# Turning half of a normalised block by VectorE squares and a trip through DRAM in place of TensorE transposes

## The chip, the cores and the metric

The kernel runs on one core of one Trainium2 chip. The time is device microseconds of one execution. The core's engines are TensorE (PE, with its weight loads shown apart as PEld), VectorE (DVE), ScalarE (ACT), GpSimd (POOL) and SyncE (SP); POOL and SP issue the DMAs.

## The reference

One decoder layer on 2048 tokens of width 1024, in float32. The output of the first sub-layer is normalised, modulated, and goes into the second:

```python
        h = x * (1.0 + sc1) + sh1
        z = h @ w_in[l]
        gate_b, gate_c, v_conv, v_pool = jnp.split(z, [CONV_CH, 2 * CONV_CH, 3 * CONV_CH], axis=-1)
        y_conv = gate_b * _short_conv(gate_c * v_conv, conv_w[l])
        y_pool = _multiscale_pool(v_pool, w_pool[l], pool_scale[l])
        mix = jnp.concatenate([y_conv, y_pool], axis=-1) @ w_out[l]
        x = _layer_norm(DEEPNORM_ALPHA * x + (1.0 + g1) * mix, ln1_g[l], ln1_b[l])

        h = x * (1.0 + sc2) + sh2
        f = jnp.square(jax.nn.relu(h @ w_mlp_in[l])) @ w_mlp_out[l]
        x = _layer_norm(DEEPNORM_ALPHA * x + (1.0 + g2) * f, ln2_g[l], ln2_b[l])
```

The hidden width of the second sub-layer is 4096. The convolution, the pooling and the scales from the conditioning vector are small beside the four matrix products.

## The kernel before

The tokens go in two blocks of 1024. In each block the input projection (`in_proj_0`, `in_proj_1`), the output projection (`out_proj`), the up-projection (`up`, eight groups of 512 hidden columns) and the down-projection (`down`) follow each other. A matrix product is made of blocks of half size with seven products in place of eight (sums of blocks stand in for one of them); keys such as "11", "22" or "1" in `ORDER` name the operand block or sum that a product takes. A float32 operand is split by `split` into a high part, cast by ACT, and a low part, subtracted by DVE, and `mm3` makes three matmuls from them. One product of the up-projection is 24 matmuls of 128x128 by 128x512.

`out_proj` gets tokens on partitions: `R[0]` to `R[7]` are eight tiles of 128 tokens by 1024 features, loaded with the residual x and added to. Its operands come from the DRAM tensor `msum` with features on partitions and tokens along the row (`Operands.begin`, `second`, `third`). `normalise` and `scale` centre and scale each finished tile and store it to `nsave`, from which the residual is read later.

The up-projection needs features on partitions again. `turned` does that. `back(0)` turns tiles 0 to 3, 32 transposes of 128x128 by TensorE with an identity, while the last product of `out_proj` runs; the results are operands "11" and "21". `back(1)` turns tiles 4 to 7 in the same way, after the first two products of the first up group; `back(2)` splits operand "22" from it, and `back(3)` to `back(6)` make the sums "1", "2", "3" and "4" with the blocks that `back(0)` stored in `hsave`. In `mlp` the order is: two products of `ups[0]`, `back(1)`, two products of `ups[1]`, `back(2)`, a product of `ups[0]` that takes "22", `back(3)`, a product that takes "1", and so on:

```python
        ups = [up(b, g, B) for g in range(NC)]
        for g in range(2):
            next(ups[g])
            back(1 + g)
        for i in range(3, 7):
            next(ups[0])
            back(i)
```

A scheduler puts each engine's instructions in a fixed order when the program is built, by its own estimate of when data is there; each engine then takes them in that order and waits for semaphores. Tiles come from pools with a fixed number of buffers: ten `o`, five `r`, six `w` and 28 `h` tiles of 1024 columns, and eight PSUM banks `ps`. DMAs that POOL issues take one of eight completion semaphores in turn, and each waits for the last holder of its own.

Of the kernel before, what the change touches and what calls it, by code (L numbers as in the profile page):

```python
# [50 lines left out]
def tile_hybrid_layer(ctx: ExitStack, tc: tile.TileContext, opening, xT, x, wada, win,  # L51
# [20 lines left out]
    def t_o(w=T, dt=F32):  # L72
        return mk(big, [P, w], dt, "o", 10)
# [13 lines left out]
    def split(src, hi, lo):  # L87
        high = nc.scalar.copy(hi, src)  # L88
        return high.ins, nc.vector.tensor_tensor(lo, src, hi.bitcast(F32), op=ALU.subtract).ins  # L89


    def mm3(ps, whi, wlo, xhi, xlo, first, last, goes_on=False):
        nc.tensor.matmul(ps, whi, xhi, start=first, stop=False, skip_group_check=goes_on)  # L93
# [97 lines left out]
    msum = tc.dram_tile([7, NG - 1, P, H], F32, name="msum")  # L191
    wosum = tc.dram_tile([2, 4, P, T], F32, name="wosum")
    udeep = tc.dram_tile([NC, P, 3 * Q], F32, name="udeep")
    wdeep = tc.dram_tile([NC, P, T + 3 * Q], F32, name="wdeep")

    def ada_first():
# [562 lines left out]
    def turned(R):  # L759
        B = {}  # L760
        raw = []

        def operand(key, q, src):
            hi, lo = t_h(), t_h()
            split(src, hi, lo)
            B[key, q] = hi, lo

        def transposed(h, k0, dst):
            for i in range(2):
                k = k0 + i  # L770
                ps = t_ps()
                for t in range(4):
                    nc.tensor.transpose(ps[:, t * P : t * P + P], R[4 * h + t][:, k * P : k * P + P], ident)  # L773
                sc, sh = lng[:, k : k + 1], lnb[:, k : k + 1]
                if h and i:
                    nc.vector.tensor_scalar(dst[:, i * H : i * H + H], ps, sc, sh, op0=ALU.mult, op1=ALU.add)
                else:
                    nc.scalar.activation(dst[:, i * H : i * H + H], ps, AF.Identity, bias=sh, scale=sc)
            return dst

        def back(h):
            if h == 0:
                for q in range(4):
                    r = transposed(0, 2 * q, t_r())
                    nc.gpsimd.dma_start(hsave[q], r)
                    operand("11" if q < 2 else "21", q % 2, r)
            elif h == 1:
                for q in range(2):
                    raw.append((transposed(1, 4 + 2 * q, t_o()), transposed(1, 2 * q, t_o())))
            elif h == 2:  # L790
                for q in range(2):
                    operand("22", q, raw[q][0])
            elif h == 3:
                for q in range(2):
                    b11 = t_o()
                    nc.sync.dma_start(b11, hsave[q])
                    tt(raw[q][1], raw[q][1], b11, ALU.subtract)
                    operand("1", q, raw[q][1])
                    raw[q] = raw[q][0], raw[q][1], b11
            elif h == 4:  # L800
                for q in range(2):
                    tt(raw[q][0], raw[q][0], raw[q][1], ALU.subtract)
                    operand("2", q, raw[q][0])
            elif h == 5:
                for q in range(2):
                    tt(raw[q][2], raw[q][0], raw[q][2], ALU.subtract)
                    operand("3", q, raw[q][2])
            else:
                for q in range(2):
                    b21 = t_o()  # L810
                    nc.sync.dma_start(b21, hsave[2 + q])
                    tt(b21, b21, raw[q][0], ALU.subtract)
                    operand("4", q, b21)

        return B, back

# [3 lines left out]
    class Operands:  # L820
# [10 lines left out]
        def begin(self, n):  # L831
            i = self.index(n)
            r = t_r()
            nc.sync.dma_start(r.rearrange("p (a n) -> p a n", a=2),
                              msum[i, 0:2].rearrange("a p n -> p a n"))
            self.a[n, 0] = parts(r)
            self.weights(n, 0)

        def weights(self, n, g, tile=None):
# [7 lines left out]
        def second(self, n):  # L847
            ns = range(n, min(n + 2, 7))
            r = t_r()
            for i, m in enumerate(ns):  # L850
                self.a[m, 1] = hi, lo = t_h(), t_h()
                nc.sync.dma_start(r[:, halves[i]], msum[self.index(m), 2])
                split(r[:, halves[i]], hi[:, :H], lo[:, :H])

        def third(self, n):
            hi, lo = self.a[n, 1]
            return split(self.mixed[self.index(n)], hi[:, H:], lo[:, H:])

        def whole(self, n):
            self.begin(n)  # L860
# [2 lines left out]
                self.second(n)  # L863
            self.third(n)

    def out_proj(b, ops):
        R, X, Y = [], {}, {}
        B, back = turned(R)
        lo_, hi_ = halves
        mv = {}  # L870
        late, begun = [], []

        def load_x():
            xt = t_o(D)
            nc.gpsimd.dma_start(xt, x[b * T + len(R) * P : b * T + len(R) * P + P, :])
            R.append(xt)

        def matmuls(n, banks, new, ks, then):
            for t in range(4):
                if new and ks[0] == 0:  # L880
# [13 lines left out]

        def end(t, cs, other, scalar=1.0):
            if t not in mv:
                mv[t] = mk(sm, [P, 8], F32, "mv", 8)
            i = 4 + cs.start // H
            begun[:] = [nc.vector.scalar_tensor_tensor(R[t][:, cs], R[t][:, cs], scalar, other, op0=ALU.mult,
                                                       op1=ALU.add, accum_out=mv[t][:, i : i + 1]).ins]  # L900

        def scale():
            t = late.pop()
            begun[:] = [nc.vector.tensor_scalar(R[t], R[t], mv[t][:, 0:1], mv[t][:, 6:7], op0=ALU.add,
                                                op1=ALU.mult).ins]
            nc.gpsimd.dma_start(nsave[t], R[t])

        def normalise(t):
            stats_act(R[t], mv[t])
            if late:  # L910
                scale()
            var_act(mv[t])
            inv_sqrt(mv[t])
            late.append(t)

        def first_row(t, ps):
            end(t, hi_, ps)
            normalise(t)
# [36 lines left out]
        matmuls(6, X, False, every, last_row)  # L955
        scale()
        return B, back

# [540 lines left out]
```

## Time and profile before

| | |
|---|---|
| median of 3 runs | 1734.65 us (1734.5 to 1736.54) |
| span of the profiled execution | 1733.2 us |
| PE busy | 1723.5 us, 7855 matmuls |
| DVE, ACT, POOL busy | 1314.6, 868.1, 205.8 us |
| mean granted TensorE clock | 0.999 |
| DMA moved | 465.24 MB, 268 GB/s |
| the 128 transposes of L773 | 15.6 us of PE |

The profiled execution's own time is given by its span, from its first to its last instruction; the runs' times are a little longer. A row of a timeline has start, duration, engine, line, operation, the tile written and the tiles read, and the shape; x32 means 32 instructions merged. A row of a group has, behind the count, busy time and mean duration in ns, and then the idle time of the engine just ahead of them with what ended it. Matmuls overlap: one lasts 0.39 us but the next starts 0.227 us later. A DMA row has KB and the median time from issue to landing.

### The profile page before, as it was taken

The numbers are of one execution on the slowest core, as the hardware profiler recorded it, in microseconds if no ns is written. First come the engines' busy times: TensorE is split into PE (matmuls) and PEld (weight loads), VectorE is DVE, ScalarE is ACT, GpSimd is POOL, SyncE is SP. The second block draws the span as 40 slices with busy tenths as digits, with TensorE's granted clock in tenths as the row PEclk, the third lists the DMA queues.
The fourth block names the chain that finished last, engine by engine and source line by source line (L and its number), as shares of the span: only waits on it lengthen the run. The fifth ranks groups of instructions, "written<-read, shape, count | busy, mean of one in ns | idle before, by whom it ended". The sixth has DMA issues, their size and how long they took to land.

```text
span 1733.2 us, 21912 instructions
## 1 busy us (share of the span) xinstructions
PE 1723.5 (99%) x7855; PEld 1435.5 (83%) x7855; DVE 1314.6 (76%) x1726; ACT 868.1 (50%) x1172; POOL 205.8 (12%) x399
## 2 busy tenths in 40 slices
PE   9999999999999999999999999999999999999998
PEld 7888888888888888888888888888888889888887
DVE  8897798877777686669686789687566778665896
ACT  6323368554445554446573344775444567444451
POOL 0222220122322000100000000102111110000000
PEclk9999999999999999999999999999999999999999
DMA  9998877778888998887572366657545589777771
GB/s 387 345 337 319 302 267 269 267 262 325 311 326 319 381 418 332 291 286 284 196 271 76 110 219 219 230 185 282 215 179 222 197 290 418 294 273 249 267 264 50
DMA packets 142685, 465.24 MB, mean 268 GB/s; under 512 B 16488, under 2 KB 17008, under 8 KB 142576
## 3 DMA queue, kind: packets, MB, share of 16 engines
q1 hardware_dynamic: 97920, 303.39, 48.0%
q0 software_dynamic: 44656, 160.46, 24.4%
q8 instruction: 61, 1.00, 0.2%
q14 instruction: 48, 0.39, 0.1%
HBM read 318.55 MB, written 145.23 MB: 268 GB/s over the span
## 4 chain that ended last, share of the span: by engine, by line
PE 95%; DMA 3%; issue 1%; DVE 1%; ACT 0%; SPq 0%; POOL 0%; DVEq 0%; POOLq 0%
PE ps L95 30%; PE ps L93 30%; PE ps L94 30%; PE ps L425 3%; DMA r<-in_w 1%; DMA usum<-o 1%; PE ps L773 1%; DVE o L98 0%; DMA o<-in_w 0%; DMA o<-in_opening 0%; DVE w L89 0%; DVE r L98 0%; ACT w L88 0%; DVE o L1369 0%; SPq L108 0%
## 5 line engine op out<-in xcount | busy, mean ns | idle before, releaser
L95 PE MATMUL ps<-h,w 128*128 128x512 f32 x1312 | 510.2, 389 | 0.4 <-DVE w L89 0.4
L94 PE MATMUL ps<-h,w 128*128 128x512 f32 x1312 | 510.3, 389 | 0.0
L93 PE MATMUL ps<-h,w 128*128 128x512 f32 x1312 | 510.0, 389 | 0.0
L93 PE MATMUL ps<-h,h 128*128 128x512 f32 (+1 forms) x1176 | 444.2, 378 | 0.0
L95 PE MATMUL ps<-h,h 128*128 128x512 f32 (+1 forms) x1176 | 444.1, 378 | 0.0
L94 PE MATMUL ps<-h,h 128*128 128x512 f32 (+1 forms) x1176 | 444.0, 378 | 0.0
L88 ACT CAST h<-r 128x1024 fp32r<-128x1024 f32 (+2 forms) x186 | 187.8, 1014 | 298.0 <-PE ps L94 186.8
L95 PEld LDWEIGHTS ps<-h,w 128*128 128x128 f32 x1312 | 246.3, 188 | 52.1 <-DVE w L89 0.8
L94 PEld LDWEIGHTS ps<-h,w 128*128 128x128 f32 x1312 | 246.3, 188 | 51.5 <-DVE h L89 0.5
L93 PEld LDWEIGHTS ps<-h,w 128*128 128x128 f32 x1312 | 246.0, 188 | 51.3 <-ACT h L88 0.2
L89 DVE TENSOR_TENSOR h<-r,h 128x1024 fp32r<-128x1024 f32 (+2 forms) x186 | 217.3, 1173 | 93.5 <-ACT h L88 93.0
L88 ACT CAST w<-r 128x1024 fp32r<-128x1024 f32 x156 | 164.3, 1053 | 242.6 <-PE ps L94 231.3
L89 DVE TENSOR_TENSOR w<-r,w 128x1024 fp32r<-128x1024 f32 x156 | 190.5, 1222 | 96.3 <-ACT w L88 95.4
L94 PEld LDWEIGHTS ps<-h,h 128*128 128x128 f32 x1176 | 221.3, 188 | 41.1
L95 PEld LDWEIGHTS ps<-h,h 128*128 128x128 f32 x1176 | 221.3, 188 | 40.8
L93 PEld LDWEIGHTS ps<-h,h 128*128 128x128 f32 x1176 | 221.3, 188 | 40.5
L98 DVE TENSOR_TENSOR o<-o,o 128x1024 f32<-128x1024 f32 (+2 forms) x193 | 171.1, 890 | 41.0 <-DMA usum<-o 31.8
L98 DVE TENSOR_TENSOR o<-o,ps 128x512 f32<-128x512 f32 (+1 forms) x175 | 113.7, 658 | 54.3 <-PE ps L95 53.4
L89 DVE TENSOR_TENSOR h<-w,h 128x1024 fp32r<-128x1024 f32 x114 | 137.6, 1207 | 4.3 <-ACT h L88 4.1
L88 ACT CAST h<-w 128x1024 fp32r<-128x1024 f32 x114 | 118.6, 1040 | 12.8 <-DMA w<-wdeep 4.1
L1013 POOL DMA_DIRECT2D usum<-o x111 | 59.4, 535 | 472.3 <-ACT o L1010 195.0
L98 DVE TENSOR_TENSOR r<-r,r 128x1024 f32<-128x1024 f32 x60 | 73.4, 1223 | 21.5 <-DMA r<-in_w 17.5
(160 smaller groups left out, 1243.0 us busy)
## 6 DMA issues: line engine op xcount, KB each, us to landing
usum<-o POOLq DMA_DIRECT2D x111, 512.0 KB, 4.8
r<-usum SPq DMA_DIRECT2D x109, 512.0 KB, 5.5
w<-w2sum SPq DMA_DIRECT2D x64, 512.0 KB, 5.9
r<-in_w SPq DMA_DIRECT2D x60, 512.0 KB, 6.0
w<-in_w SPq DMA_DIRECT2D x40, 512.0 KB, 7.4
o<-in_w SPq DMA_DIRECT2D x72, 256.0 KB, 6.4
w2sum<-o POOLq DMA_DIRECT2D x64, 256.0 KB, 6.7
msum<-o POOLq DMA_DIRECT2D x18, 512.0 KB, 4.9
```

Of the source, the lines that this page charges most:

```text
L88: high = nc.scalar.copy(hi, src)
L89: return high.ins, nc.vector.tensor_tensor(lo, src, hi.bitcast(F32), op=ALU.subtract).ins
L93: nc.tensor.matmul(ps, whi, xhi, start=first, stop=False, skip_group_check=goes_on)
L94: nc.tensor.matmul(ps, whi, xlo, start=False, stop=False, skip_group_check=goes_on)
L95: nc.tensor.matmul(ps, wlo, xhi, start=False, stop=last, skip_group_check=goes_on)
L98: return nc.vector.tensor_tensor(out_, a, b_, op=op)
L425: nc.tensor.matmul(ps[m, h], wt[:, w : w + P], A[k][p // 2][:, hs], start=k == 0 and p == 0, stop=k == KD - 1 and p == 2)
L773: nc.tensor.transpose(ps[:, t * P : t * P + P], R[4 * h + t][:, k * P : k * P + P], ident)
L1013: nc.gpsimd.dma_start(usum[g, i], r)
```

## The change

The four tiles of the second half of a block are no longer turned by TensorE. When such a tile is scaled, DVE turns it in squares of 32x32 into four collecting tiles (`blocks`, one for each 256 features), four instructions a tile. After the last tile 16 DMAs store them into the new DRAM tensor `tsave`, in pieces of 512 bytes, and `back(1)` loads them back with features on partitions, four DMAs of 512 KB. Scale and shift by `lng` and `lnb` are then applied to the loaded tile, half by ACT and half by DVE, where they were applied to the PSUM banks.

For the squares to land in token order the rows of an `R` tile are other tokens than before: partition group `a` of tile `t` holds 32 tokens that lie 128 apart from the next group's (`rows_of`). So the tile is loaded and stored by four DMAs of 32 rows each, and the operands from `msum` are split with their columns in another order (`split_rows`, 512 columns at a time). The first half is still turned by TensorE and put back into token order as it leaves PSUM.

```diff
+    def by_rows(ap):
+        return ap.rearrange("p (t a j) -> p a t j", t=4, a=4)
+    def by_tokens(ap):
+        return ap.rearrange("p (a t j) -> p a t j", t=4, a=4)
+    def split_rows(src, hi, lo):
+        for i in range(0, src.shape[-1], H):
+            cs = slice(i, i + H)
+            split(by_tokens(src[:, cs]), by_rows(hi[:, cs]), by_rows(lo[:, cs]))
...
+    tsave = tc.dram_tile([4, 2, P, H], F32, name="tsave")
...
-        def transposed(h, k0, dst):
-            for i in range(2):
+        blocks = []
+
+        def turn(t):
+            if t == 0:
+                blocks.extend(t_o() for _ in range(4))
+            for q, r in enumerate(blocks):
+                nc.vector.transpose(r.rearrange("p (b t j) -> p t b j", b=8, t=4)[:, t],
+                                    R[4 + t][:, q * Q : q * Q + Q].rearrange("p (b j) -> p b j", b=8))
+                if t == 3:
+                    for a in range(4):
+                        own = slice(32 * a, 32 * a + 32)
+                        nc.gpsimd.dma_start(
+                            tsave[q].rearrange("k (q i) (a r) -> a i (k q) r", q=4, a=4)[a],
+                            r[own].rearrange("i (b r) -> i b r", b=8))
+
+        def affine_row(dst, src, k):
+            sc, sh = lng[:, k : k + 1], lnb[:, k : k + 1]
+            nc.scalar.activation(dst, src, AF.Identity, bias=sh, scale=sc)
+
+        def turned_back(k0, dst):
+            nc.gpsimd.dma_start(dst.rearrange("p (k n) -> p k n", k=2), tsave[k0 // 2].rearrange("k p n -> p k n"))
+            for i, hs in enumerate(halves):
                 k = k0 + i
+                if i:
+                    nc.vector.tensor_scalar(dst[:, hs], dst[:, hs], lng[:, k : k + 1], lnb[:, k : k + 1],
+                                            op0=ALU.mult, op1=ALU.add)
+                else:
+                    affine_row(dst[:, hs], dst[:, hs], k)
+            return dst
+
+        def transposed(k0, dst):
+            for i, hs in enumerate(halves):
                 ps = t_ps()
                 for t in range(4):
-                    nc.tensor.transpose(ps[:, t * P : t * P + P], R[4 * h + t][:, k * P : k * P + P], ident)
...
+                    nc.tensor.transpose(ps[:, t * P : t * P + P], R[t][:, (k0 + i) * P : (k0 + i) * P + P], ident)
+                affine_row(by_tokens(dst[:, hs]), by_rows(ps), k0 + i)
...
-                    raw.append((transposed(1, 4 + 2 * q, t_o()), transposed(1, 2 * q, t_o())))
+                    raw.append((turned_back(4 + 2 * q, t_o()), turned_back(2 * q, t_o())))
...
-            self.a[n, 0] = parts(r)
+            self.a[n, 0] = hi, lo = t_h(), t_h()
+            split_rows(r, hi, lo)
...
+    def rows_of(t):
+        for a in range(4):
+            start = t // 4 * H + a * P + t % 4 * 32
+            yield slice(start, start + 32), slice(32 * a, 32 * a + 32)
...
-            nc.gpsimd.dma_start(xt, x[b * T + len(R) * P : b * T + len(R) * P + P, :])
+            for rs, own in rows_of(len(R)):
+                nc.gpsimd.dma_start(xt[own], x[b * T + rs.start : b * T + rs.stop, :])
...
-            nc.gpsimd.dma_start(nsave[t], R[t])
+            for rs, own in rows_of(t):
+                nc.gpsimd.dma_start(nsave[rs.start // P, rs.start % P : rs.start % P + 32], R[t][own])
+            if t >= 4:
+                turn(t - 4)
```

Three places in the built order of block 0, each before and after. First POOL, where the output projection ends and the up-projection begins. Before, `o_1969` to `o_1975` are tiles 4 to 7 and `o_2483` is the first result of the up-projection:

```order
L785 DMA hsave<-r_2325 128x1024
L906 DMA nsave<-o_1969 128x1024
L906 DMA nsave<-o_1971 128x1024
L906 DMA nsave<-o_1973 128x1024
L906 DMA nsave<-o_1975 128x1024
L1013 DMA usum<-o_2483 128x1024
```

After, from the third collecting tile `o_2444` on, with what each row waits for (DMASW0 to DMASW7 are the eight semaphores of POOL's DMAs; the four tiles' stores and the first two collecting tiles' stand ahead of it in the same way). `o_2622` and `o_2630` become operand "22", `o_2626` and `o_2634` operand "1":

```order
L791 DMA tsave<-o_2444 32x8x128 [waits DMASW4_49,DVE_49]
L791 DMA tsave<-o_2444 32x8x128 [waits DMASW5_49]
L791 DMA tsave<-o_2444 32x8x128 [waits DMASW6_49]
L791 DMA tsave<-o_2444 32x8x128 [waits DMASW7_49]
L791 DMA tsave<-o_2445 32x8x128 [waits DMASW0_49,DVE_49]
L791 DMA tsave<-o_2445 32x8x128 [waits DMASW1_49]
L791 DMA tsave<-o_2445 32x8x128 [waits DMASW2_49]
L791 DMA tsave<-o_2445 32x8x128 [waits DMASW3_49]
L1060 DMA usum<-o_2582 128x1024 [waits DMASW4_49,DVE_49,Activation_49]
L800 DMA o_2622<-tsave 128x2x512 [waits DMASW7_49,DMASW6_49,DMASW5_49]
L800 DMA o_2626<-tsave 128x2x512
L800 DMA o_2630<-tsave 128x2x512 [waits DMASW2_49,DMASW3_49,DMASW1_49,DMASW0_49]
```

Between the tiles' stores and the later results there are now 16 stores, one result's store and four loads, and the first load waits for the third collecting tile's stores to land.

Second ACT, at the affine and the cast of operand "22". Before, `o_2523` and `o_2549` are "22", `w_2657` the weight that it is multiplied with, `w_2703` and `w_2748` the next two:

```order
L88 CAST w_2657<-r_2655 128x1024
L778 ACTIVATE o_2523<-ps_2524,lnb,lng 128x512
L1009 ACTIVATE o_2483<-o_2483 128x1024
L778 ACTIVATE o_2536<-ps_2537,lnb,lng 128x512
L1010 ACTIVATE o_2483<-o_2483 128x1024
L778 ACTIVATE o_2549<-ps_2550,lnb,lng 128x512
L778 ACTIVATE o_2562<-ps_2563,lnb,lng 128x512
L88 CAST h_2647<-o_2523 128x1024
L88 CAST h_2651<-o_2549 128x1024
L1000 COPY o_2607<-ps_2581 128x512
L88 CAST w_2703<-r_2701 128x1024
```

After, `w_2720`, `w_2766` and `w_2811` are these three weights:

```order
L88 CAST w_2675<-r_2673 128x1024
L88 CAST w_2720<-r_2718 128x1024
L88 CAST w_2766<-r_2764 128x1024
L88 CAST w_2811<-r_2809 128x1024
L797 ACTIVATE o_2622<-o_2622,lnb,lng 128x512
L88 CAST h_2710<-o_2622 128x1024
L797 ACTIVATE o_2626<-o_2626,lnb,lng 128x512
L1047 COPY o_2670<-ps_2644 128x512
L1047 COPY o_2670<-ps_2657 128x512
L797 ACTIVATE o_2630<-o_2630,lnb,lng 128x512
L88 CAST h_2714<-o_2630 128x1024
```

The casts of the weights for the next two products moved ahead of the affine of "22", and the copies of `ups[1]`'s banks (into `o_2670`) behind it.

Third PE, where `ups[1]`'s second product ends and the product with "22" begins. Before:

```order
L93 MATMUL ps_2629<-h_2339,w_2612 128x512
L94 MATMUL ps_2629<-h_2340,w_2612 128x512
L95 MATMUL ps_2629<-h_2339,w_2613 128x512
L93 MATMUL ps_2661<-h_2647,w_2657 128x512
L94 MATMUL ps_2661<-h_2648,w_2657 128x512
L95 MATMUL ps_2661<-h_2647,w_2658 128x512
```

After, `h_2710` and `h_2711` are the high and low part of "22":

```order
L104 MATMUL ps_2692<-h_2390,w_2675 128x512
L105 MATMUL ps_2692<-h_2391,w_2675 128x512
L106 MATMUL ps_2692<-h_2390,w_2676 128x512
L104 MATMUL ps_2724<-h_2710,w_2720 128x512
L104 MATMUL ps_2737<-h_2710,w_2720 128x512
L105 MATMUL ps_2724<-h_2711,w_2720 128x512
```

The product with "22" follows `ups[1]`'s directly, as before; nothing was moved in between, and the 32 transposes that stood ahead of `ups[1]` are gone (7819 rows before, 7755 now, in both blocks together).

More of the change, by code (lines that the diff above doesn't have):

```diff
@@ L766, in operand @@
             B[key, q] = hi, lo
-        def transposed(h, k0, dst):
-            for i in range(2):
-                k = k0 + i
+        blocks = []
[17 more added lines that the diff above has]
+            for i, hs in enumerate(halves):
+                k = k0 + i
+                if i:
[6 more added lines that the diff above has]
+            for i, hs in enumerate(halves):
                 ps = t_ps()
                 for t in range(4):
[L773 to L778, printed above, removed]
+                    nc.tensor.transpose(ps[:, t * P : t * P + P], R[t][:, (k0 + i) * P : (k0 + i) * P + P], ident)
+                affine_row(by_tokens(dst[:, hs]), by_rows(ps), k0 + i)
             return dst
@@ L783, in back @@
                 for q in range(4):
-                    r = transposed(0, 2 * q, t_r())
+                    r = transposed(2 * q, t_r())
                     nc.gpsimd.dma_start(hsave[q], r)
@@ L813, in back @@
                     operand("4", q, b21)
-        return B, back
+        return B, back, turn
     class Operands:
@@ L852, in second @@
                 nc.sync.dma_start(r[:, halves[i]], msum[self.index(m), 2])
-                split(r[:, halves[i]], hi[:, :H], lo[:, :H])
+                split_rows(r[:, halves[i]], hi[:, :H], lo[:, :H])
         def third(self, n):
             hi, lo = self.a[n, 1]
-            return split(self.mixed[self.index(n)], hi[:, H:], lo[:, H:])
+            return split_rows(self.mixed[self.index(n)], hi[:, H:], lo[:, H:])
         def whole(self, n):
@@ L864, in whole @@
             self.third(n)
+    def rows_of(t):
+        for a in range(4):
+            start = t // 4 * H + a * P + t % 4 * 32
+            yield slice(start, start + 32), slice(32 * a, 32 * a + 32)
     def out_proj(b, ops):
         R, X, Y = [], {}, {}
-        B, back = turned(R)
+        B, back, turn = turned(R)
         lo_, hi_ = halves
```

## The prediction, on record before the run

> **What bounds the kernel now.** The page first: span, busy engines, the chain that ended last.
>
> ```profile
> span 1733.2 us, 21912 instructions
> ...
> PE 1723.5 (99%) x7855; PEld 1435.5 (83%) x7855; DVE 1314.6 (76%) x1726; ACT 868.1 (50%) x1172; POOL 205.8 (12%) x399
> ...
> PE 95%; DMA 3%; issue 1%; DVE 1%; ACT 0%; SPq 0%; POOL 0%; DVEq 0%; POOLq 0%
> ```
>
> TensorE (PE) is busy for 1723.5 of 1733.2 us and carries 95% of the chain: about 10 us in the whole run are not PE's. Whatever PE no longer does comes off the end, and whatever PE is made to wait for goes on. So I read PE's timeline where the change takes its work away, at the end of block 0's output projection, and the same place in block 1.
>
> ```profile
> 269.40 0.39 PE L93 MATMUL ps<-h,w 128*128 128x512 f32 x1
> ...
> 280.29 3.71 PE L773 MATMUL ps<-ident,o 128*128 128x128 f32 x32
> 283.75 0.47 PE L93 MATMUL ps<-h,w 128*128 128x512 f32 x1
> ...
> 294.53 0.39 PE L95 MATMUL ps<-h,w 128*128 128x512 f32 x1
> ...
> 1126.53 3.70 PE L773 MATMUL ps<-ident,o 128*128 128x128 f32 x32
> ```
>
> The up-projection's first two products run from 269.40 to 280.29 (48 matmuls, 0.227 us each), then the 32 transposes that the change removes, then `ups[1]`'s two products from 283.75 to about 294.8. Only then does PE ask for operand "22", the first made from these transposes. Before, it was ready long ago:
>
> ```profile
> 278.57 0.81 DVE L904 TENSOR_SCALAR o<-o,mv 128x1024 f32<-128x1024 f32 x1
> ...
> 286.85 2.36 DVE L89 TENSOR_TENSOR h<-o,h 128x1024 fp32r<-128x1024 f32 x2 [1.41 <-ACT h L88]
> ...
> 285.77 2.00 ACT L88 CAST h<-o 128x1024 fp32r<-128x1024 f32 x2
> ...
> 276.93 0.53 POOL L906 DMA_DIRECT2D nsave<-o  x1 [1.23 <-DVE mv L737]
> ```
>
> The last of the four normalised tiles is scaled at 278.57 + 0.81 = 279.4, and both halves of "22" are split by 286.85 + 2.36 = 289.2, 5.6 us before PE's demand. The fourth row is POOL's store of the tile before the last, at 276.93.
>
> **The change, part by part.**
>
> *Removed.* 32 transposes a block: 283.75 − 280.29 = 3.46 us of PE, and block 1's row reads the same (3.70 with its pipelined tail). Nothing else waits for them, so PE gains 2 × 3.5 = 7 us and the demand for "22" moves from 294.8 to 291.2.
>
> *Added, with a price each:*
>
> ```profile
> L773 PE MATMUL ps<-ident,o 128*128 128x128 f32 x128 | 15.6, 275 | 0.0
> ...
> L98 DVE TENSOR_TENSOR o<-o,o 128x256 f32<-128x256 f32 x24 | 10.2, 423 | 0.6
> L904 DVE TENSOR_SCALAR o<-o,mv 128x1024 f32<-128x1024 f32 x16 | 13.0, 811 | 3.1 <-ACT mv L741 2.9
> L776 DVE TENSOR_SCALAR o<-ps,lng,lnb 128x512 f32<-128x512 f32 x8 | 5.9, 804 | 0.0
> L778 ACT ACTIVATE o<-ps,lnb,lng 128x512 f32<-128x512 f32 x8 | 6.0, 772 | 0.0
> L88 ACT CAST h<-o 128x1024 fp32r<-128x1024 f32 x20 | 20.8, 1050 | 11.8 <-DVE o L98 11.8
> L89 DVE TENSOR_TENSOR h<-o,h 128x1024 fp32r<-128x1024 f32 x20 | 24.3, 1221 | 4.1 <-ACT h L88 4.1
> L89 DVE TENSOR_TENSOR h<-r,h 128x512 fp32r<-128x512 f32 x14 | 9.5, 686 | 0.2 <-ACT h L88 0.2
> L906 POOL DMA_DIRECT2D nsave<-o x16 | 8.6, 536 | 57.6 <-DVE mv L750 18.4 <-DVE mv L738 15.2 <-DVE o L904 11.0
> L356 POOL DMA_DIRECT2D msum<-o x18 | 13.0, 721 | 167.4 <-DVE o L276 105.1 <-DVE o L281 36.6 <-DVE o L98 25.2
> ```
>
> - 16 VectorE (DVE) turns of 128x256 a block. No row shows one. Bounds: 0.20 us (a quarter of L904's 0.811, a one-input pass) and 0.80 (L776, twice the columns out of PSUM). I take 0.42, the 128x256 row: 6.7 us a block, of which the eight for the last two tiles (3.4 us) follow the last scaling in DVE's order.
> - *Weighed against the skill.* 32 PE transposes take 3.46 us here, 0.11 us each. The Trainium skill, "VectorE: DVE Perf Modes", section "The three transpose paths", gives 390 ns for TensorE and 311 ns for VectorE on 128x128 bf16, so there the swap looks cheap; the trace has PE at far less than that. An estimate by that page is 2 × 311 ns for a turn of 256 columns, 0.2 us more than I take, and with eight of them on the path in each block the sum would be 3 us longer.
> - Splits of msum operands cut in two (seven a block): 2 × 0.686 against 1.22 on DVE, 0.15 us each, about 1 us a block, and as little on ACT. PE waited for neither in the out-projection; I put nothing down. The permuted views have no row; from no cost to twice the pass they stay off PE's path unless DVE falls behind (a rival below).
> - Eviction of the kept transposes writes permuted; the second half's affine passes read SBUF and not PSUM. Same number, taken at L776 and L778.
> - GpSimd (POOL): tile loads and stores become four each (+48 +48 issues in all), tsave adds 32 stores and 8 loads. An issue takes 0.54 (L906, 128 pieces) or 0.72 (L356, 256 pieces, as a tsave store has).
>
> - Tile loads in the out-projection: the eighth tile of block 0 already came 0.4 us late for DVE, which PE did not feel; three more issues add at most 1.6 us, once. I take nothing.
>
> ```profile
>   DMA o<-in_x: 0.4, 1
> ```
>
> *The path that decides.* "22" now goes scale, turn, sixteen stores, load, affine, split. On POOL all of it stands behind the four-fold stores of tiles 6 and 7, and a DMA waits for the one eight before it (one of eight semaphores each, as the order shows), so POOL's pace is the larger of its issue time and an eighth of a landing. How long landings take there (median us from issue to landing, the first two rows in 268 to 292, the next two in block 1's 1115 to 1137, then over the whole run; then minimum, median and maximum for nsave in 245 to 300 and for msum; last, windows with the busy us of PE, weight loads, DVE, ACT and POOL, the clock, and the DMA share and GB/s):
>
> ```profile
> nsave<-o POOLq DMA_DIRECT2D x4, 512.0 KB, 7.4
> ...
> o<-hsave SPq DMA_DIRECT2D x2, 512.0 KB, 6.0
> ...
> nsave<-o POOLq DMA_DIRECT2D x4, 512.0 KB, 5.2
> ...
> o<-hsave SPq DMA_DIRECT2D x2, 512.0 KB, 7.3
> ...
> r<-msum SPq DMA_DIRECT2D x14, 512.0 KB, 5.5
> ...
> DMA to landing us min/median/max: 2.9/5.3/9.6
> ...
> DMA to landing us min/median/max: 2.8/5.3/12.3
> ...
> 240.00:250.00 10.00, 10.00 (x46) 8.29 (x45) 9.76 (x29) 8.54 (x26) 2.72 (x5) 1.00 0.48 188
> ...
> 270.00:280.00 10.00, 10.00 (x46) 8.29 (x45) 7.98 (x20) 8.18 (x25) 1.93 (x4) 1.00 0.94 329
> 280.00:290.00 10.00, 10.00 (x62) 8.71 (x61) 7.16 (x8) 8.71 (x11) 0.74 (x2) 1.00 0.97 322
> 290.00:300.00 10.00, 10.00 (x46) 8.29 (x45) 9.62 (x10) 6.85 (x8) 0.53 (x1) 1.00 0.27 94
> ```
>
> The DMA engines are 97% busy until 290 and 27% after. A 512 KB store lands in 7.4 us in block 0's stretch and 5.2 in block 1's; a quarter of it less. I take 6 us in flight: 0.75 us a DMA, about the issue time.
>
> Block 0: tile 6's first store at 278 (it was at 276.9; eight turns, 3.4 us, come ahead of it, and DVE was idle for 2.0 of the ten us from 270). From it to the twelfth tsave store, which completes the piece loaded first, are 4 + 4 + 12 = 20 DMAs: 15 us, 293. It lands 5.2 later (298.2). POOL waits for that, issues the load (0.7), and the load lands after 5.5 (msum's row, 2 KB pieces too): 304.4. ACT's affine and cast, 0.77 + 1.05: 306.2. PE has waited since 291.2: 15 us. Behind it a tail: DVE must do two affines, the low part, then the second half and three subtractions for operand "1", and each product's 12-matmul half covers only 2.7 us. DVE's 4 × 1.2 against 2.7 costs some 2 us, the first low part 1: tail 3. Block 0 loses 18 us. Block 1 has the same order and quicker landings: 16.
>
> Who stands behind the waits: on POOL `ups[1]`'s stores; on ACT and DVE the reading of `ups[1]`'s banks, which PE needs back only one product later; on SP, operand "1"'s reload of hsave takes the buffers of the turned tiles and waits for tsave's stores, with weights behind it that PE uses three products on. These cost nothing beyond the tail while PE itself waits.
>
> On ACT and DVE the weights' casts for the *third* product from there (`w_2811`) now stand ahead of "22"'s affine, and their buffer comes free only when PE has finished `ups[1]`, at 291.2. So even with the data there at once PE waits: cast 1.05, affine 0.77, cast 1.05, to 294.1, 2.9 us, plus tail.
>
> Ends. Low: issues at 0.54 from 276.9, landings at the least in the rows (2.9 and 2.8): 295.7, so 4.5 + 2.5 of tail, 7 a block. High: pace 7.4 / 8 = 0.93 from 279.7, landings 7.4 and 7.3: 315.5, 24 + 4, 28 a block.
>
> **Sum**, against the profiled execution's span: − 7 + 18 + 16 = + 27, 1733.2 → 1760. The runs' median, 1734.65, stands 1.4 above that span: 1762. Low: − 7 + 14 = + 7, 1742. High: − 7 + 56 = + 49, 1784.
>
> *A second rule weighed.* The rows give 5 to 7 us for a landing beside SP's loads. The Trainium skill, "DMA: Bandwidth & Descriptors", section "Anatomy of one DMA — SWDGE (gpsimd) path", fits 2.0 us plus bytes over 436 GB/s: an estimate of 2.3 us for a tsave store and 3.2 for a load. By it POOL paces at 0.72, the load lands at 298.6, a block loses about 12 us with its tail and the time is 1752; the trace, with its stores at 5.2 to 7.4, is longer than the page's 3.2 for 512 KB.
>
> **Rivals.**
> - *The detour arrives in time* (faster). The first load would have to land by about 289.4 (291.2 less affine and cast), 10 us after the last scaling. For it: POOL is only 12% busy and the DMAs are idle after 290. Against it: 20 DMAs at the least issue time alone are 10.8 us, plus two landings, and ACT's queue holds the affine behind `w_2811`. It gives 1734.65 − 7 = 1727.7.
> - *Only the queue order binds*: landings at their minimum, POOL without slack, and the weights' casts set the wait: 4 to 7 a block, 1736 to 1742.
> - *The 512-byte pieces, or DVE, cost more than I take.* A turn at 0.8 puts 6.4 us behind the last scaling, and DVE falls behind in the out-projection too, where it is busy for 9.76 of 10 us from 240. Against it: a slow turn overlaps POOL's tile stores. At 30 a block, two more than my upper end, it gives 1734.65 − 7 + 60 = 1788.
> - *The change doesn't do what it says*: excluded, since PE's order has 64 rows fewer and nothing stands in their place.
>
> **Chances.** My forecast's range (1742 to 1784): 0.82. Queue order only (1736 to 1742): 0.06. In time: 0.05. Above 1784: 0.07. Runs of this kernel differ by about 0.2% (3.5 us), and less than that can't be told from no change: faster 0.05, same 0.02, slower 0.93. Range 1742 to 1784.
>
> **What would show it.** After: L773's group halves (15.6 to about 7.8 us); PE idles in two stretches, each 10 to 20 us, released by ACT's or DVE's split of "22"; POOL's tsave stores spread over 11 to 15 us; the tsave loads issue near 299 and land near 304. It is wrong if the loads land before 291, or if PE idles first at `ups[0]`'s or `ups[1]`'s products, waiting for a weight's low part that DVE does after the turns.

## The result and the profile after

The changed kernel takes 1779.22 us (median of 4 runs, 1777.94 to 1779.6) against 1734.58: a ratio of 1.0251, 95% interval 1.0237 to 1.0266. It is 44.6 us slower; 27.4 had been forecast, and the time lies near the upper end of the range. The page after, the same lines as before:

```profile
span 1776.2 us, 22074 instructions
...
PE 1728.6 (97%) x7791; PEld 1431.4 (81%) x7791; DVE 1323.0 (74%) x1772; ACT 872.0 (49%) x1186; POOL 278.1 (16%) x535
...
PE 90%; DVE 3%; DMA 3%; ACT 2%; issue 1%; POOL 1%; DVEq 0%; SPq 0%; ACTq 0%; POOLq 0%
```

The profiled execution is 43.0 us longer. PE is idle for 47.6 us of the span where it was idle for 9.7. In the chain PE's share falls from 95% to 90%, DVE's rises from 1% to 3% and ACT's from 0% to 2%; DMA keeps its 3%. TensorE's timeline, read at the first matmul of each stage, says where:

| stage | before | after | difference |
|---|---|---|---|
| start to block 0's first up matmul | 269.40 | 269.62 | + 0.2 |
| block 0, up-projection | 309.14 | 330.33 | + 21.2 |
| block 0 down, block 1 input projection | 457.12 | 457.27 | + 0.2 |
| block 1, output projection | 79.98 | 81.99 | + 2.0 |
| block 1, up-projection | 308.42 | 327.75 | + 19.3 |
| block 1 down, to the last matmul | 301.65 | 301.65 | 0 |

So nearly all of it lies in the two places that the prediction named. TensorE's waits there (what waits, for whom; us in total, times, longest), and its timeline:

```profile
PE ps L104 <- ACT h L88: 31.5, 2, 16.2
```

```profile
276.12 0.50 PE L104 MATMUL ps<-h,w 128*128 128x512 f32 x1 [0.82 <-ACT w L88]
...
283.48 0.50 PE L104 MATMUL ps<-h,w 128*128 128x512 f32 x1 [0.60 <-ACT w L88]
...
294.74 0.39 PE L106 MATMUL ps<-h,w 128*128 128x512 f32 x1
310.42 1.22 PE L104 MATMUL ps<-h,w 128*128 128x512 f32 x2 [15.29 <-ACT h L88]
...
322.36 0.50 PE L105 MATMUL ps<-h,w 128*128 128x512 f32 x1 [0.76 <-DVE h L89]
...
1177.50 1.22 PE L104 MATMUL ps<-h,w 128*128 128x512 f32 x2 [16.18 <-ACT h L88]
```

Operand "22" is what PE waits for, 15.29 and 16.18 us. Ahead of that it waits twice for a weight's cast, at products of `ups[0]` and `ups[1]` (276.12 and 283.48, with the low parts 2.35 us in all): the prediction had named such a wait as a sign of error, and in block 0 it comes, but PE would otherwise only have waited longer for "22". Measured from the first up matmul, "22" starts after 25.36 us before (294.76 − 269.40) and after 40.80 now: + 15.4. From there to the down-projection it was 283.78 us and is 289.53: + 5.8. Block 1 has 25.36 to 38.29 and 283.06 to 289.46: + 12.9 and + 6.4.

GpSimd's timeline through the detour, then the rows of the turns and stores over the run (ns: minimum, median, maximum), the median landing times of tsave's sixteen stores and four loads in 275 to 312, and the affine pass that the first load releases:

```profile
279.02 3.91 POOL L951 DMA_DIRECT2D nsave<-o  x8 [1.52 <-DVE o L948]
285.41 0.63 POOL L791 DMA_DIRECT2D tsave<-o  x1 [2.48 <-DMA nsave<-o]
286.70 4.05 POOL L791 DMA_DIRECT2D tsave<-o  x7 [0.66 <-DMA nsave<-o]
...
293.36 1.29 POOL L791 DMA_DIRECT2D tsave<-o  x2 [0.22 <-issue]
295.08 2.59 POOL L791 DMA_DIRECT2D tsave<-o  x4 [0.44 <-issue]
298.20 0.58 POOL L1060 DMA_DIRECT2D usum<-o  x1 [0.53 <-DMA tsave<-o]
300.75 1.44 POOL L800 DMA_DIRECT2D o<-tsave  x2 [1.97 <-DMA tsave<-o]
```

```profile
L786 DVE STREAM_TRANSPOSE o<-o x32: 390/404/445, 273.0 to 1152.1; 128x256 f32<-128x256 f32 x32
```

```profile
L791 POOL DMA_DIRECT2D tsave<-o x32: 584/584/627, 285.4 to 1165.1; - x32
```

```profile
tsave<-o POOLq DMA_DIRECT2D x16, 128.0 KB, 5.9
o<-tsave POOLq DMA_DIRECT2D x4, 512.0 KB, 7.5
```

```profile
308.48 0.81 ACT L797 ACTIVATE o<-o,lnb,lng 128x512 f32<-128x512 f32 x1 [12.49 <-DMA o<-tsave]
```

The windows (columns as in the prediction: busy us of PE, weight loads, DVE, ACT, POOL; clock; DMA share; GB/s):

```profile
285.00:290.00 5.00, 5.00 (x23) 4.12 (x24) 2.36 (x2) 2.82 (x3) 3.92 (x7) 1.00 1.03 402
...
295.00:300.00 5.00, 0.13 (x1) 0.00 (x0) 1.23 (x1) 0.98 (x1) 2.90 (x5) 0.95 1.03 399
...
305.00:310.00 5.00, 0.00 (x0) 0.00 (x0) 0.66 (x2) 1.49 (x2) 0.70 (x1) 0.50 1.03 418
310.00:315.00 5.00, 4.54 (x10) 3.15 (x11) 4.89 (x7) 4.93 (x8) 0.00 (x0) 0.50 0.25 94
```

From 285 to 310 the DMA engines are full (0.98 to 1.03, 370 to 418 GB/s), where before the change they were 27% busy from 290 to 300. All sixteen stores and the first two loads of the detour land in this stretch. And after the idle time PE's clock is 0.50.

### The profile page after: what moved, and what is told of

It is laid out like the page before. It is cut to its first block, busy times and chain, and to the rows that moved or that the text cites. A ratio compares the mean times of both kernels' runs of the same rounds, so it can differ in the third digit from the quotient of the medians.

```text
span 1776.2 us, 22074 instructions
## 1 busy us (share of the span) xinstructions
PE 1728.6 (97%) x7791; PEld 1431.4 (81%) x7791; DVE 1323.0 (74%) x1772; ACT 872.0 (49%) x1186; POOL 278.1 (16%) x535
## 4 chain that ended last, share of the span: by engine, by line
PE 90%; DVE 3%; DMA 3%; ACT 2%; issue 1%; POOL 1%; DVEq 0%; SPq 0%; ACTq 0%; POOLq 0%
PE ps L104 29%; PE ps L106 29%; PE ps L105 29%; PE ps L437 2%; DMA tsave<-o 1%; DVE o L109 1%; DVE h L89 1%; DMA o<-tsave 1%; DMA nsave<-o 1%; ACT tmp L764 1%; ACT h L88 1%; POOL nsave L951 0%; DVE w L89 0%; DVE o L948 0%; ACT r L797 0%
## 5 line engine op out<-in xcount | busy, mean ns | idle before, releaser
L88 ACT CAST h<-r 128x1024 fp32r<-128x1024 f32 (+1 forms) x200 | 189.2, 956 | 304.4 <-PE ps L105 179.2
L89 DVE TENSOR_TENSOR h<-r,h 128x1024 fp32r<-128x1024 f32 (+1 forms) x200 | 218.4, 1101 | 91.5 <-ACT h L88 91.1
```

## The experiments

**The permutation without the detour** (`e1_perm`). Tiles 4 to 7 are turned by TensorE again, out of permuted rows; the fourfold loads and stores of the tiles stay:

```diff
         def turned_back(k0, dst):
-            nc.gpsimd.dma_start(dst.rearrange("p (k n) -> p k n", k=2), tsave[k0 // 2].rearrange("k p n -> p k n"))
             for i, hs in enumerate(halves):
+                ps = t_ps()
+                for t in range(4):
+                    nc.tensor.transpose(ps[:, t * P : t * P + P], R[4 + t][:, k * P : k * P + P], ident)
...
-            if t >= 4:
-                turn(t - 4)
```

> The permuted rows, the four-fold tile loads and stores and the permuted splits stay; the second half is turned by TensorE again and nothing goes through tsave. Theory: the detour is the loss (24.7 and 22.8 us in the two up-projections of the changed kernel, less 3.5 each for the transposes), and the permutation costs only the 2.0 us by which block 1's output projection got longer (79.98 to 81.99 us): 1736 to 1738 us. Rival: those 2.0 us come from the turns or from the detour's traffic too, and the permutation is free: 1734 to 1735.5 us. Second rival: the permuted views or the extra issues cost time at several places, 1740 us and more.

Measured: 1756.62 us, ratio 1.0125 (1.011 to 1.014). The number falls to the second rival: the permuted rows with their fourfold DMAs alone cost 21.7 us. By stages it is 14.6 in block 0's up-projection (323.72 for 309.14), 3.3 in block 1's and 1.9 in block 1's output projection. GpSimd's window and SP's issues of the up weights, first in this kernel and then in the one before:

```profile
250.00:260.00 10.00, 9.99 (x58) 8.02 (x58) 6.25 (x18) 6.06 (x15) 10.00 (x19) 1.00 0.84 284
```

```profile
270.36 7.69 SPq L561 DMA_DIRECT2D r<-in_w  x3
```

```profile
250.00:260.00 10.00, 9.99 (x61) 8.44 (x60) 7.29 (x17) 6.44 (x14) 4.86 (x9) 1.00 0.81 327
```

```profile
261.31 5.74 SPq L550 DMA_DIRECT2D r<-in_w  x3
```

POOL is busy for all ten us, where it was for 4.86, and the up weights are issued 9 us later. I read the link as the `r` buffers, which come free when hsave's stores have landed; that link itself is not shown, but the next run takes the extra issues away.

**The same, with each tile stored as it lies** (`e9_perm_nat`; the token order is put right when the residual goes to `rsave`, four DMAs each, in the down-projection):

```diff
-            for rs, own in rows_of(t):
-                nc.gpsimd.dma_start(nsave[rs.start // P, rs.start % P : rs.start % P + 32], R[t][own])
+            nc.gpsimd.dma_start(nsave[t], R[t])
...
-            nc.gpsimd.dma_start(rsave[t], r)
+            for rs, own in rows_of(t):
+                nc.gpsimd.dma_start(rsave[rs.start // P, rs.start % P : rs.start % P + 32], r[own])
```

> As e1_perm (permuted rows, TensorE transposes, no tsave), but the normalised tiles are stored to nsave as they lie, by one plain DMA of 128 rows, and put into token order when the residual is stored to rsave in the down-projection (four DMAs there). The tile loads stay fourfold. Theory (GpSimd's queue): without the 48 extra issues the hsave stores go out near 257 to 264 us as in the kernel before, the r buffers and the weights come as early as there, and block 0's up-projection loses its 14.6 us and block 1's its 3.3: 1735 to 1738 us, of which up to 1.9 are the output projection of block 1 with its fourfold loads. Rival: the permuted splits and evictions, or another order of ScalarE and VectorE that they bring, cost the time: 1748 us or more.

Measured: 1739.68 us, 1.0031 (1.0019 to 1.0044), 1.7 above the expected range. SP's first weights go out at 262.64, near the 261.31 of the kernel before. So 16.9 of the 21.7 us were the fourfold stores to `nsave` on GpSimd's queue; the permuted splits, the evictions, the fourfold loads and the fourfold stores to `rsave` cost 4.9 together, 1.6 of it in block 1's output projection.

**One DMA a tile with a three-level pattern** (`e5_perm_one` without the detour, `e6_one` with it):

```diff
-            for rs, own in rows_of(len(R)):
-                nc.gpsimd.dma_start(xt[own], x[b * T + rs.start : b * T + rs.stop, :])
+            nc.gpsimd.dma_start(xt, rows_of(x[b * T : b * T + T, :], len(R)))
...
+    def rows_of(src, t):
+        return src.rearrange("(h a t i) d -> h t a i d", h=2, a=4, t=4)[t // 4, t % 4]
```

> As e1_perm (permuted rows, TensorE transposes, no tsave), but each tile is loaded and stored by one DMA with a three-level access pattern and not by four. Theory: what e1_perm lost is GpSimd's queue. In 250 to 260 us GpSimd is busy all ten us there, the four hsave stores go out at 262.9 to 265.9 us where they went at 257.1 to 263.9 before, their r buffers come free later and the weights and later hsave reloads behind them come late: with one DMA in place of four the time is back at 1734 to 1737 us. Rival: the permuted splits, evictions or the order that they bring cost the 20 us, then it stays at 1750 us or more.

> The whole change (turns, tsave, permutation), but each tile is loaded and stored by one DMA and not by four. Theory (GpSimd's queue): two tile stores and not eight stand ahead of tsave's stores, which start near 282 us and not 285.4, the weights come as early as before, and operand 22's product starts 4 to 5 us sooner in each block, with a tail of up to 6 us behind it as before; block 1's output projection gets its 2 us back: 1764 to 1769 us. Rival (bandwidth): the bytes are the same and the DMA engines are full from 285 to 310, so nothing moves but the 2 us: 1774 to 1779 us.

Measured: 1806.9 and 1841.86 us (1.0415 and 1.0619). Far above the theory in both, with a cause that neither rival named: the new DMAs themselves were slow. Landing of the tile loads (minimum, median, maximum) in `e6_one`, then in the changed kernel:

```profile
DMA to landing us min/median/max: 9.3/18.4/30.1
```

```profile
DMA to landing us min/median/max: 2.6/5.7/10.9
```

512 KB in one DMA land in 18.4 us (16.2 in `e5_perm_one`); 128 KB, four of which make a tile, in 5.7. How much of the time lost these landings explain was not measured. These runs say nothing on GpSimd's queue, and `e9_perm_nat` and `e10_nat` took their place.

**The whole change with the plain stores** (`e10_nat`, the same edit as `e9_perm_nat`).

> The whole change, with the stores to nsave as in e9_perm_nat: one plain DMA a tile ahead of tsave's stores in place of four. Theory (GpSimd's queue and two landings behind it): tsave's first store goes out near 282 us and not 285.4, operand 22's product starts about 4.5 us earlier in each block, as it did in e2_hold (305.9 for 310.4), and nothing is given back at the next product since the tiles' buffers are not held: 1764 to 1770 us. Rival (the DMA engines' rate from 285 to 310 us decides): 1774 to 1779 us.

Measured: 1776.23 us, 1.0241 (1.0225 to 1.0256): 3.0 below the change, in the rival's range. In block 0 "22" starts 40.78 us after the first up matmul, as before (40.80). With the weights there in time, DVE does their low parts ahead of the last turns, which end at 287.6 and not at 282.1:

```profile
286.15 1.42 DVE L786 STREAM_TRANSPOSE o<-o 128x256 f32<-128x256 f32 x4
```

```profile
311.70 1.22 PE L104 MATMUL ps<-h,w 128*128 128x512 f32 x2 [18.79 <-ACT h L88]
```

PE's waits for weights (2.35 us) are gone, and its wait for "22" is 3.5 us longer. Block 1 gains 2.0 us there (36.33 for 38.29). The 17 us of the fourfold stores are thus no part that adds up: in the changed kernel they lie under the detour. What the detour costs is shown by this run and `e9_perm_nat`, which differ only in it: 1776.23 − 1739.68 = 36.6 us.

**The stores of tiles 4 to 7 behind the detour** (`e2_hold`):

```diff
+            if t < 4:
+                save_rows(R, t)
+            else:
+                turn(t - 4)
...
                     raw.append((turned_back(4 + 2 * q, t_o()), turned_back(2 * q, t_o())))
+                for t in range(4, 8):
+                    save_rows(R, t)
```

> The sixteen nsave stores of tiles 4 to 7 are put behind the loads of the turned tiles in GpSimd's order; nothing else changes. Theory (a serial chain through GpSimd's order): the first tsave store goes out when tile 7 is turned, near 281.5 us and not at 285.4, the twelfth near 290 and not at 294.6, the two landings stay near 6 and 7 us, and the product that takes operand 22 starts 4 to 5 us earlier in each block: 1769 to 1771 us. Rival (the DMA engines, 98 to 103 per cent busy at about 400 GB/s from 285 to 310 us, set the landings): only the 1 MB of tiles 6 and 7 moves out of the way, 2.6 us at that rate, and what is issued earlier lands no earlier: 1774 to 1779 us.

Measured: 1779.92 us, 1.0263 (1.0246 to 1.028): no gain. The theory's step holds and its sum does not:

```profile
305.92 1.22 PE L104 MATMUL ps<-h,w 128*128 128x512 f32 x2 [10.84 <-ACT h L88]
...
323.38 1.22 PE L104 MATMUL ps<-h,w 128*128 128x512 f32 x2 [9.53 <-ACT h L88]
```

```profile
289.16 27.14 SPq L562 DMA_DIRECT2D r<-w1sum  x4
316.47 0.81 SPq L835 DMA_DIRECT2D o<-hsave  x2
```

"22" starts 4.5 us earlier in block 0 and 2.8 in block 1, but in block 0 PE then waits 9.53 us for operand "1". The reload of hsave that "1" needs goes out at 316.5 (297.9 in the changed kernel). In SyncE's order it now stands behind a fourth weight load, and SyncE waits 18.4 us there until VectorE has taken the low part of a weight (SyncE's waits from 300 to 320):

```profile
SPq L562 <- DVE w L89: 18.4, 1, 18.4
```

Nor did the landings stay as they were. The twelfth tsave store is issued at 287.7 (294.1 in the changed kernel), 6.4 us earlier, but takes longer to land, first here and then in the changed kernel:

```profile
DMA to landing us min/median/max: 8.1/8.1/8.1
```

```profile
DMA to landing us min/median/max: 6.1/6.1/6.1
```

**The pieces of "22" first** (`e12_nat_first`, on `e10_nat`):

```diff
-            for q, r in enumerate(blocks):
+            for q, r in sorted(enumerate(blocks), key=lambda e: (e[0] + 2) % 4):
...
-                for q in range(2):
-                    raw.append((turned_back(4 + 2 * q, t_o()), turned_back(2 * q, t_o())))
+                lower = [turned_back(4 + 2 * q, t_o()) for q in range(2)]
+                raw.extend((lower[q], turned_back(2 * q, t_o())) for q in range(2))
```

> e10_nat with the pieces of operand 22 first: the third and fourth collecting tiles are turned and stored ahead of the first and second, and their two loads are issued first and second, not first and third. The bytes and the number of DMAs are the same. Theory (the place in GpSimd's order sets operand 22): eight stores and not twelve stand at the head of the first load's wait, 4 x 0.65 = 2.6 us, and the second load no longer stands behind another operand's; the waits for operand 22 (18.8 and 14.4 us) fall by 2.5 to 4 us each and as much of it stays: 1768 to 1771 us. Rival (the DMA engines' rate, or the chain behind the product of operand 22, decides): what is gained ahead of operand 22 comes back as a wait at the next product, operand 1, whose pieces are now last: 1774 to 1778 us.

Measured: 1777.4 us, 1.0243 (1.0226 to 1.026): the rival's range. GpSimd's loads, their landing and the first affine pass, then the landing in `e10_nat`:

```profile
299.38 2.14 POOL L800 DMA_DIRECT2D o<-tsave  x3 [0.20 <-issue]
```

```profile
o<-tsave POOLq DMA_DIRECT2D x4, 512.0 KB, 9.2
```

```profile
308.20 0.81 ACT L797 ACTIVATE o<-o,lnb,lng 128x512 f32<-128x512 f32 x1 [15.24 <-DMA o<-tsave]
```

```profile
o<-tsave POOLq DMA_DIRECT2D x4, 512.0 KB, 7.6
```

The first load goes out 1.4 us earlier from the first up matmul (299.38 − 270.11 for 301.64 − 270.92), and three are now in flight together; the affine pass comes 0.75 us earlier, since the four loads take 9.2 us (median) to land and not 7.6. Block 1 gains nothing either (36.85 us to "22", 36.33 in `e10_nat`). What is gained ahead of the DMA engines is given back in them. The return at operand "1" that the rival named is not seen. Outside this chain, at 542 us, PE waits 1.86 us for a weight's low part, so the profiled execution is no shorter than that of `e10_nat`.

**Issue by ScalarE** (`e3_act_queue`): `nc.scalar.dma_start` in place of `nc.gpsimd.dma_start` for tsave's stores and loads.

> The stores to tsave and the loads from it are issued by ScalarE and not by GpSimd, so they stand behind no tile store and no GpSimd semaphore. Serial theory: in block 1 the first store goes out near 1152.5 us and not at 1155.05, the issues no longer take 0.65 us each behind one another's semaphores, the wait of PE in block 1 falls from 16.2 to about 10 us; in block 0 a weight's cast for the second group stands behind the affine passes in ScalarE's order, so the wait moves forward and is shorter in sum too: 1765 to 1772 us. Rival (bandwidth): the same bytes share the same DMA engines, landings get as much longer as the issue gets earlier, 1777 to 1781 us.

Measured: 1788.39 us, 1.0306 (1.029 to 1.0321), slower than either theory. ScalarE's queue in block 1 and TensorE in block 0:

```profile
1158.16 12.89 ACTq L791 DMA_DIRECT2D tsave<-o  x16
```

```profile
310.29 0.79 PE L104 MATMUL ps<-h,w 128*128 128x512 f32 x1 [27.36 <-ACT w L88]
```

The stores land sooner (3.6 us median in block 1, 5.5 in the changed kernel), but the sixteen issues hold ScalarE for 12.89 us, and casts and affine passes stand behind them. In block 0 PE waits 27.36 us for a weight's cast at the second group. The run does not tell the two theories apart.

**PE kept busy in the gap** (`e4_warm`):

```diff
+        x = B["11", 0][0]
+        for _ in range(64 // 16):
+            spare = t_ps()
+            for _ in range(16):
+                nc.tensor.matmul(spare, x[:, :P], x[:, :H], start=True, stop=True)
```

> As the changed kernel, with 64 matmuls of 128x512 more in each block that feed nothing (14.5 us at 0.227 us each), placed between the second group's first two products and the product that takes operand 22, where PE waits for 15.3 and 16.2 us. Theory: after its idle time PE runs at half its clock for about 6 us (granted clock 0.50, one matmul each 0.425 us from 310.4 to 316.5), which costs 3 us a block; with PE busy the clock stays at 1.00 and the time falls by 6 us to about 1773 us, though the data come no earlier. Rival: the slow matmuls wait for operands or weights and the clock row only goes with the idle time: no change, 1779 us. If the extra matmuls run past the landing: up to 1 us longer.

Measured: 1778.94 us, 1.0254 (1.0239 to 1.027): the rival's answer, for a reason that it did not give. The clock did stay up:

```profile
312.22 0.73 PE L104 MATMUL ps<-h,w 128*128 128x512 f32 x2 [1.49 <-ACT h L88]
```

```profile
310.00:315.00 5.00, 2.74 (x12) 1.62 (x10) 3.56 (x6) 4.43 (x7) 0.00 (x0) 1.00 0.58 224
```

From the product of "22" to the down-projection it takes 288.71 and 289.12 us in the two blocks, against 289.53 and 289.46: 0.8 and 0.3 less, not 3. At full clock PE waits for DVE's and ACT's splits instead (0.77, 0.53 and 1.37 us in block 0, where the changed kernel has one wait of 0.76); the low clock covered waits that are there anyway.

**Cover by other products** (`e7_one_fill2`, and the control `e8_before_fill2`): product 1 of groups 2 and 3 ahead of "22".

```diff
+        if g in EARLY:
+            r = t_r()
+            nc.sync.dma_start(r, w1[g][1])
+            seven(iter([r]), B)(1, Y, True)
+            save(keep(Y), 1)
+            yield
         product(0, X, True)
         c11 = keep(X)
+        if g in EARLY:
+            y = t_o()
+            nc.sync.dma_start(y, usum[g, 1])
+            tt(c11, c11, y, ALU.add)
```

> e6_one, and one product each of the third and fourth up group (those that take operands 11 and 21 alone) is done ahead of the product that takes operand 22, kept in DRAM and added later: 48 matmuls, 10.9 us of PE work in each block's gap, at the price of one more 512 KB load, store and addition for each. Theory: only the wait for operand 22 and its tail cost time, so with a wait of 10 to 13 us in e6_one these 10.9 us take nearly all of it; e6_one less 18 to 24 us, 1742 to 1750 us, and down to 1730 if the tail goes too. Rival: the detour's DMAs get later by the additional traffic, as fast as the cover grows, or the additions cost DVE time that PE waits for: 1755 us and more.

> The same rearrangement of the up groups in the kernel before, without turns, tsave or permutation: the control for e7_one_fill2. Theory: PE does the same matmuls in another order and waits for nothing there, 1734 to 1737 us. Rival: the additional loads, stores and additions make PE wait somewhere, 1740 us or more.

Measured: 1865.22 and 1767.49 us. The control is 32.4 us slower than the kernel before (1.0187, 1.0171 to 1.0202), its longest wait 6.4 us for PSUM banks that ScalarE reads; and the base of `e7_one_fill2` carries the slow DMAs. That a cover would save the change was not shown.

**The transposes alone** (`e11_free`): the kernel before without the 32 transposes of each block. The second half is not turned at all: its operands are made from the first half's turned tiles, loaded from hsave.

> The kernel before, with the 32 TensorE transposes of the second half of each block left out and the operands made from the first half's turned tiles (loaded from hsave early) in their place; no turns, no tsave, no permutation. It leaves the turning of the second half out: the price of the removed transposes alone. Theory: 3.5 us of PE a block and no wait: 1727 to 1729 us. Rival: the 3.5 us also cover the weights' casts or the reading of PSUM banks, so that less comes back: 1730 to 1735 us.

Measured: 1743.53 us, 1.0051 (1.0036 to 1.0066), 8.7 above the kernel before and outside both ranges.

```profile
297.75 0.79 PE L94 MATMUL ps<-h,w 128*128 128x512 f32 x1 [4.28 <-DVE h L89]
```

```profile
294.28 1.23 DVE L98 TENSOR_TENSOR o<-o,o 128x1024 f32<-128x1024 f32 x1 [2.24 <-DMA o<-hsave]
```

The low part of "22"'s second half stands in DVE's order behind a subtraction that waits for an hsave reload; PE waits 4.28 and 4.38 us for it. The 7 us could not be priced apart from the order that the edit brings.

## Why the prediction was right or wrong

- *Sign, place and mechanism: right.* PE idles in two stretches, released by the split of "22", and the detour does not arrive in time. The rivals "in time" and "only queue order" are out, the one above 1784 was not reached.
- *The size: short by 16 us, inside a wide range.* The span was to grow by 27 us and grew by 43.0. In block 0 the wait for "22" is 3.9 us longer than the sum has it and the tail 2.8; in block 1 they are 3.4 and 3.4; 2.0 lie in block 1's output projection, which had no term. All these errors go the same way, and the upper end of 28 us a block is what kept the time in the range.
- *Turns and stores: right.* 0.40 us (0.42 taken); an issue is cheaper, 0.58 (0.72), but sixteen stores take 12.3 us, 0.77 each (0.75 taken).
- *The removed transposes: not confirmed as a gain.* TensorE's transposes take 8.7 us where they took 15.6, so the work is gone. But the weights' waits ahead of "22" use 2.35 of the 3.5 us in block 0, what is left only makes the wait for "22" longer, and in `e11_free` such 3.5 us did not come back.
- *"The path that decides": the chain is right, two links are too short.* In block 0: tile 6's first store 279.0 (278), the twelfth tsave store from 294.0 to 294.7 (293), first load 300.75 (298.2), data 308.5 (304.4), PE 310.4 (306.2). GpSimd's order is not what holds the first load: the sixteen stores and one usum store ahead of it are issued by 298.78, and GpSimd then sits idle for 1.97 us until the twelfth store has landed, 6.1 us after its issue and not 5.2. And the load takes 7.0 us from the end of its issue to the affine pass, not 5.5: I took the median of the `msum` loads over the whole run and the windows of *before*, in which the DMA engines are 27% busy from 290 to 300, while the late weights, the hsave reloads and the detour's own 4 MB now fill just that stretch. In `e12_nat_first` an issue 1.4 us earlier bought 0.75 us, in `e2_hold` one 6.4 us earlier bought 4.5. This is the 4 us in block 0. The second rule that was weighed (the Trainium skill, "DMA: Bandwidth & Descriptors", section "Anatomy of one DMA — SWDGE (gpsimd) path") gave estimates of 2.3 us for a store and 3.2 for a load; the medians here are 5.9 and 7.5, so beside this traffic the trace does not agree with it.
- *The tail: mis-sized.* 3 us taken, 5.8 and 6.4 measured. The halved clock is in it but explains under 1 us (`e4_warm`).
- *Fourfold loads and stores: no cost outside the chain was taken, which is wrong as a step.* By themselves, with TensorE's transposes kept, the fourfold stores cost 17 us, and the weights go out 9 us later. In the changed kernel they lie under the detour and only about 3 us show (`e10_nat`), 0.5 of it in the output projection of block 1, whose 2.0 us had no term.

What stays open: how far the landings are the DMA engines' rate and how far latency. That a store issued earlier took 8.1 us and not 6.1 (`e2_hold`) speaks for the rate, but every reordering moved something else, and no run took the weights' traffic away from the detour. What the detour would cost with PE covered is open too.

## What to carry to other kernels

A trip through DRAM on the path is two landings plus a queue, and the landings are to be taken from the traffic that will be there after the change, not from the stretch as it was: a stall moves other loads into it. That a queue has slack on average does not make it free to split its DMAs in four; look at who gets buffers back from that queue. Shortening one link of such a chain paid here only where the next link was not already due, so read the next two waits ahead of counting a gain.

## What was unexpected of the hardware

- The same 512 KB took 18.4 us to land (median, `e6_one`) with an outermost level of four, and 5.6 us as 128 plain rows in the kernel before. The Trainium skill, "DMA: Bandwidth & Descriptors", section "Why a DMA increments its semaphore by 16 and not by 1", says that the slowest dimension sets how many of the 16 engines a DMA uses, so four here. The trace agrees: the eighth tile's load runs alone in both kernels, and its packets of 4 KB, 0.16 us each, are 4 in flight at a time in `e6_one` and 16 in the kernel before. The windows in it, first `e6_one`, then before (DMA share and GB/s are the last two):

```profile
257.00:262.00 5.00, 0.00 (x0) 0.00 (x0) 1.01 (x3) 1.17 (x3) 0.00 (x0) 0.76 0.21 81
```

```profile
238.00:239.00 1.00, 1.00 (x6) 0.84 (x5) 1.00 (x2) 0.97 (x3) 0.00 (x0) 1.00 0.98 369
```

- After some 15 us without work PE's matmuls came 0.425 us apart and not 0.227, at a granted clock of 0.50, for about 6 us (310.4 to 316.5). Its price here was under 1 us a block.
